# Prompt attention in a hybrid decoder step: TensorE's order written out by hand, value products of two steps in one run, probabilities turned in place, one ring of PSUM banks, and 640 keys cut as 384 and 256

## The chip, the cores and the metric

The program runs on one core of one Trainium2 chip. The metric is device time in microseconds (us) of one execution; the figure for the kernel before is the median of three runs. TensorE does the matrix products and the transposes, VectorE and ScalarE empty PSUM and do the softmax, GpSimd scales the probabilities in SBUF, and SyncE issues most of the transfers.

## The reference, cut to what matters

The reference is one layer of a decoder with 1024 prompt tokens and 32 sample tokens: input projections, sparse attention with an indexer, retention, and gated output products. What the change touches is the attention of the prompt and, in one line, the indexer's scores.

```python
def index_scores(qi, wi, ki):
    s = jnp.einsum('bqhd,bsd->bqhs', qi.astype(jnp.float32), ki.astype(jnp.float32))
    ...
    return jnp.einsum('bqhs,bqh->bqs', jax.nn.relu(s), w)

def sparse_attend(q, kg, vg, valid):
    logits = jnp.einsum('bqhd,bqkhd->bhqk', q, kg) * HEAD_DIM_A ** -0.5
    logits = jnp.where(valid[:, None], logits, -jnp.inf)
    p = jax.nn.softmax(logits, axis=-1)
    return jnp.einsum('bhqk,bqkhd->bqhd', p, vg)
```

Queries come in 8 blocks of 128, and block b sees (b + 1) * 128 keys. The kernel doesn't gather keys: it computes all logits of a block and adds a bias that masks those not selected.

## The kernel before, in words

The program is written with a tile framework that keeps the program's data dependences and chooses each engine's order itself, by a planner that simulates the program. `tc.issue_after(ins)` adds one constraint: what is traced inside the block and runs on the engine of `ins` comes after `ins`. All engines work through their order one by one, so an instruction that waits holds what stands behind it.

The stage of the change works on 4 pairs of heads `p`. For each, the 8 query blocks are taken in the order 7, 0, 6, 1 and 5, 2, 4, 3, two to a step, so that each step has 9 blocks of 128 keys for each of two heads. That makes 16 steps. A step has three parts.

- `logits` (L1319): for each block and head, the keys are cut in banks of up to 512 columns. Each bank takes two products (L1334 with the high part of the queries, L1335 with the low part) into a PSUM bank of the ring `lg` (three banks). VectorE adds the bias and keeps the running extreme (L1336), writing to the SBUF tile `lg` (three buffers); ScalarE takes the exponential with its row sum (L1342), VectorE the reciprocal (L1347), GpSimd scales in place (L1350). A generator yields after each bank: six to a step. 640 keys are cut as 512 and 128.
- `turn` (L1354): 18 transposes of 128x128 (L1362), four to a PSUM bank of the ring `tr` (two banks, for the last half step group also three of `lg`); ScalarE and VectorE copy each bank to an SBUF tile `pT` (L1365), every third copy on VectorE.
- `combine` (L1367): 18 products of turned probabilities with values, recorded as 36 instructions since fp32 products have two records each (L1380), 64 columns of the array for each head, into the bank `po` (one bank, kept for two steps). `together` ties them behind the first one. After every second step VectorE multiplies by the gate `za` (L1387) and splits the result in two parts (L1097, L1098).

Between these lies other work for TensorE: `from_retention` makes output products of the retention branch, 24 pieces of 12 products with 352 columns (L1131 to L1133) into a bank `pj` of two, and VectorE merges each piece (L1418). Five pieces are in the prologue, beside the logits of steps 0 and 1, one is left for after the last step.

In the loop over steps the program traces `turn`, for some steps a piece, the operand loads of the next pair, `combine`, the logits of the step two ahead, and one more piece up to step 11. The planner interleaves these on TensorE as their banks come free. PSUM holds 3 `lg`, 2 `tr`, 1 `po` and 2 `pj` banks.

After the stage, tiles `t` and `u` are loaded over the stage's freed SBUF (`load_merged`, L1471) and the attention branch's output products follow in the same pieces, merged on VectorE at L1520.

The indexer (L880 to L895) computes scores for blocks 7 to 2 in the first 130 us, four heads each, cut in banks of 512 and the rest (L887, L888), and ScalarE reads both banks at once (L890).

Of the kernel before, what the change touches and what calls it, by code (L numbers as in the profile page):

```python
# [8 lines left out]
F32 = mybir.dt.float32  # L9
# [3 lines left out]
AF = mybir.ActivationFunctionType  # L13
OP = mybir.AluOpType
# [5 lines left out]
T = 1024  # L20
# [104 lines left out]
def _hybrid_step(ctx, tc, A, outs, dbg):  # L125
    nc = tc.nc
# [24 lines left out]
    def pl():  # L151
        return ps.tile([128, 1024], F32, name="pl", bufs=2)
# [4 lines left out]
    def two():  # L157
        return [ps.tile([128, 512], F32, name="pb", bufs=3) for _ in (0, 1)]
# [26 lines left out]
    def together(products):  # L185

        last = first = products[0]()
        with tc.issue_after(first.ins):
            for f in products[1:]:
                last = f()  # L190
        return last
# [53 lines left out]
    def last_on(engine):  # L245
        return next(i for i in reversed(nc.cur_bb.bb.instructions) if i.engine == engine)
# [577 lines left out]
    with ExitStack() as s1:  # L824
# [4 lines left out]
        with ExitStack() as s2:  # L829
# [50 lines left out]
            for b in range(7, 1, -1):  # L880
                W = (b + 1) * 128
                for h in range(4):
                    p = pl()
                    for n0 in range(0, W, 512):
                        n1 = min(W, n0 + 512)
                        q = QS[h][:, b * 128:b * 128 + 128]
                        nc.tensor.matmul(p[:, n0:n1], q, KH[:, n0:n1], start=True, stop=False)  # L887
                        nc.tensor.matmul(p[:, n0:n1], q, KL[:, n0:n1], start=False, stop=True)  # L888
                    rl = ip.tile([128, LK], F32, name="rl", bufs=2)
                    nc.scalar.activation(rl[:, :W], p[:, :W], AF.Relu)  # L890
                    if h == 0:
                        nc.vector.tensor_scalar(SC[b], rl[:, :W], wsc[:, b, 0:1], None, op0=OP.mult)
                    else:
                        scored = nc.vector.scalar_tensor_tensor(SC[b], rl[:, :W], wsc[:, b, h:h + 1], SC[b], op0=OP.mult, op1=OP.add)
                if b == 7:  # L895
                    whole_row = scored.ins
                nc.vector.tensor_add(SC[b][:, W - 128:W], SC[b][:, W - 128:W], C[:, C_CAUS:C_CAUS + 128])
# [189 lines left out]
    def pbank(name, bufs):  # L1087
        return ps.tile([128, 512], F32, name=name, bufs=bufs)
# [6 lines left out]
    def parts(dst, src):  # L1095

        nc.scalar.copy(dst[0], src)  # L1097
        nc.vector.tensor_sub(dst[1], src, f32(dst[0]))  # L1098
# [59 lines left out]
    asked = {}  # L1158
# [160 lines left out]
    def logits(ap, step):  # L1319

        blocks, ops = step["blocks"], step["ops"][0]
        lg = step["lg"] = ap.tile([128, 2, 9 * 128], F32, name="lg", bufs=3)
        scaled_ = []
        c0 = 0
        for b in blocks:
            W = (b + 1) * 128
            qb = slice(b * 128, b * 128 + 128)
            st = ap.tile([128, 2, 4], F32, name="st", bufs=12)
            for i, (k, qh, ql) in enumerate(ops):
                l = lg[:, i, c0:c0 + W]  # L1330
                for n0 in range(0, W, 512):
                    n1 = min(W, n0 + 512)
                    x = pbank("lg", 3)
                    nc.tensor.matmul(x[:, :n1 - n0], qh[:, qb], k[:, n0:n1], start=True, stop=False)  # L1334
                    nc.tensor.matmul(x[:, :n1 - n0], ql[:, qb], k[:, n0:n1], start=False, stop=True)  # L1335
                    step["masked"] = nc.vector.tensor_tensor_reduce(  # L1336
                        out=l[:, n0:n1], in0=x[:, :n1 - n0], in1=BI[b][:, n0:n1], scale=-0.125,
                        scalar=-BIGNEG if n0 == 0 else st[:, i, 0:1], op0=OP.add, op1=OP.min,
                        accum_out=st[:, i, 0:1] if n1 < W else st[:, i, 1:2]).ins
                    if n1 < W:  # L1340
                        yield
                nc.scalar.activation(l, l, AF.Exp, bias=st[:, i, 1:2], scale=-1.0, accum_out=st[:, i, 3:4])  # L1342
                yield
            scaled_.append((st, c0, W))
            c0 += W
        for st, c0, W in scaled_:
            nc.vector.reciprocal(st[:, :, 2], st[:, :, 3])  # L1347
            for i in (0, 1):
                l = lg[:, i, c0:c0 + W]
                nc.gpsimd.tensor_scalar(l, l, st[:, i, 2:3], 0.5, op0=OP.mult, op1=OP.mult)  # L1350
# [3 lines left out]
    def turn(ap, step):  # L1354

        lg = step["lg"]
        PT = step["PT"] = []
        for j0 in range(0, 18, 4):
            m = min(4, 18 - j0)
            x = pbank("lg", 3) if step["p"] == 3 and step["group"][0] == 5 and j0 in (4, 8, 12) else pbank("tr", 2)  # L1360
            for j in range(j0, j0 + m):
                step["turned"] = nc.tensor.transpose(x[:, 128 * (j - j0):128 * (j - j0) + 128], lg[:, j % 2, 128 * (j // 2):128 * (j // 2) + 128], ident)  # L1362
            flip[0] += 1
            PT.append(ap.tile([128, 512], F32, name="pT", bufs=5))
            step["copied"] = (nc.vector.tensor_copy if flip[0] % 3 == 0 else nc.scalar.copy)(PT[-1][:, :128 * m], x[:, :128 * m])  # L1365

    def combine(ap, step):  # L1367

        (b0, b1), p, PT = step["blocks"], step["p"], step["PT"]
        ops, V, za = step["ops"]  # L1370
        if step["half"] == 0:
            step["po"][0] = pbank("po", 1)
        po = step["po"][0]

        slot = {b: i for i, b in enumerate(sorted(step["group"]))}
        run = [(b1, kb, b0 + 1 + kb) for kb in range(b1, -1, -1)] + [(b0, kb, kb) for kb in range(b0 + 1)]

        def product(b, kb, j, i):
            r = slice(64 * i, 64 * i + 64)
            return nc.tensor.matmul(po[r, 128 * slot[b]:128 * slot[b] + 128], V[:, kb, r], PT[j // 2][:, 256 * (j % 2) + 128 * i:256 * (j % 2) + 128 * i + 128],  # L1380
                                    start=(kb == (b if b == b1 else 0)), stop=(kb == (0 if b == b1 else b)))
        step["last"] = together([lambda b=b, kb=kb, j=j, i=i: product(b, kb, j, i) for b, kb, j in run for i in (1, 0)])
        if step["half"] == 1:
            pick = slice(0, 4, 3) if 0 in step["group"] else slice(1, 3)
            two = lambda t: t.rearrange("p (g c) -> p g c", c=256)[:, pick]
            y = ap.tile([128, 2, 256], F32, name="y", bufs=1)
            nc.vector.tensor_tensor(y, po.rearrange("p (g c) -> p g c", c=256), two(za), op=OP.mult)  # L1387
            parts((two(yah[:, p, :T]), two(yal[:, p, :T])), y)

    RT = dram.tile([D, TT], F32, name="RT")  # L1390

# [1 line left out]
    with ExitStack() as s4:  # L1393
# [4 lines left out]
        def operands(p):  # L1398
            if p not in loaded:
                loaded[p] = pair_operands(ap, p)  # L1400
            return loaded[p]
# [20 lines left out]

        for j in range(3):
            load_gate(j)
        steps = []
        for p in range(4):
            for group in ((7, 0, 6, 1), (5, 2, 4, 3)):
                po = [None]
                for half in (0, 1):
                    steps.append(dict(p=p, group=group, blocks=group[2 * half:2 * half + 2], half=half, po=po))  # L1430
        side = (x for j in range(KT) for x in from_retention(j))
        next(side)
        for step in steps[:2]:
# [8 lines left out]
                    next(side)  # L1442
            for _ in banks:
                pass
        for s_, step in enumerate(steps):
            if s_ == 4:
                nc.sync.dma_start(zs, by_pair(ZD))
                with tc.issue_after(step["masked"]):
                    nc.vector.tensor_tensor(YS, YS, zs, op=OP.mult)
                    parts((yah[:, :, T:], yal[:, :, T:]), YS)  # L1450
            turn(ap, step)
            if s_ >= 14 or s_ < 4:
                with tc.issue_after(step["turned"].ins):
                    next(side)
            if s_ % 4 == 0 and step["p"] + 1 < 4:
                with tc.issue_after(asked[3].ins):
                    operands(step["p"] + 1)
            combine(ap, step)
            if s_ + 2 < len(steps):
                steps[s_ + 2]["ops"] = operands(steps[s_ + 2]["p"])  # L1460
                for _ in logits(ap, steps[s_ + 2]):
                    pass
            with tc.issue_after(steps[max(s_ - 1, 0)]["last"].ins):
                for _ in zip(range(int(s_ <= 11)), side):
                    pass
        last = steps[-1]["last"]
    mp_ = ExitStack()
    mp = mp_.enter_context(tc.tile_pool(name="mp", bufs=1, side="right", reuse_waits="tile"))
    merged = {}
# [181 lines left out]
```

## Time and profile before

| | us |
|---|---|
| median of 3 runs | 1096.48 (1096.37 to 1097.05) |
| profiled execution, its own time | 1097.52 |
| its span, first to last instruction | 1095.7 |
| TensorE busy, matmuls | 1077.7 |
| VectorE busy | 669.9 |
| ScalarE busy | 468.7 |
| GpSimd busy | 230.0 |
| stage of the change (797.5 to 948.2 of the span) | 150.7 |

The profiled execution is 1.04 us above the median and lies 1.82 us above its own span. Matmuls are pipelined: a record is longer than the time after which the next one starts, so the distance between two starts is what a product costs, and a wait shorter than a record's end doesn't show as idle time.

### The profile page before, as it was taken

How to read it: one execution, taken by the hardware profiler on the slowest of the kernel's cores; microseconds unless marked ns; L12 is line 12 of the kernel's file. 1: busy time of each engine (PE TensorE's matmuls, PEld its weight loads, DVE VectorE, ACT ScalarE, POOL GpSimd, SP SyncE). 2: the span in 40 equal slices, each digit the busy share in tenths (PEclk: the TensorE clock that was granted, in tenths of full speed). 3: DMA queues.
4: the chain of work that ended last, by engine and by line, in shares of the span. 5: the costliest groups of instructions: out<-in, count | busy, mean ns of one | idle time of the engine just before them, and what ended most of it. 6: DMA issues, size and time to landing. Idle time of an engine off the chain costs nothing. (4 is left out here: it accounts for less than half of the span.)

```text
span 1095.7 us, 20456 instructions
## 1 busy us (share of the span) xinstructions
PE 1077.7 (98%) x8159; PEld 985.8 (90%) x8159; DVE 669.9 (61%) x1538; ACT 468.7 (43%) x925; POOL 230.0 (21%) x195
## 2 busy tenths in 40 slices
PE   7999999999999999999999999999999999999997
PEld 6899799999999989999999998888899998998776
DVE  6875269698887868999133222211266767497665
ACT  5675355455555555232244233311245666443211
POOL 0013025014321220020322222244122343100000
PEclk9999999999999999999999999999999999999999
DMA  9924344264254515522886758386887531457431
GB/s 296 265 73 126 95 118 138 84 197 127 80 161 128 157 47 184 156 83 100 289 278 206 240 168 248 122 286 228 311 296 239 188 114 31 144 187 249 163 116 58
DMA packets 156196, 185.64 MB, mean 169 GB/s; under 512 B 18740, under 2 KB 127172, under 8 KB 155012
## 3 DMA queue, kind: packets, MB, share of 16 engines
q1 hardware_dynamic: 145728, 147.81, 42.7%
q0 software_dynamic: 9856, 35.66, 9.7%
q8 instruction: 64, 1.05, 0.4%
q10 hardware_dynamic: 516, 0.86, 0.2%
q14 instruction: 32, 0.26, 0.1%
HBM read 139.34 MB, written 41.17 MB: 165 GB/s over the span
## 5 line engine op out<-in xcount | busy, mean ns | idle before, releaser
L226 PE MATMUL pj<-hh,wh 128*128 128x352 f32 (+1 forms) x1168 | 382.7, 328 | 0.0
L227 PE MATMUL pj<-hl,wh 128*128 128x352 f32 (+1 forms) x1168 | 378.8, 324 | 0.0
L228 PE MATMUL pj<-hh,wl 128*128 128x352 f32 (+1 forms) x1168 | 378.2, 324 | 0.2 <-POOL wl L212 0.2
L226 PEld LDWEIGHTS pj<-hh,wh 128*128 128x128 f32 x1168 | 219.3, 188 | 8.4 <-issue 7.1
L227 PEld LDWEIGHTS pj<-hl,wh 128*128 128x128 f32 x1168 | 219.8, 188 | 6.8 <-issue 6.0
L228 PEld LDWEIGHTS pj<-hh,wl 128*128 128x128 f32 x1168 | 219.4, 188 | 3.8 <-issue 3.2
L978 DVE TENSOR_SCALAR_CACHE_REDUCE eq<-sc,cand 128x896 bf16<-128x896 f32 (+4 forms) x155 | 135.7, 876 | 2.5
L211 ACT CAST wh<-ws 128x1024 fp32r<-128x1024 f32 (+1 forms) x65 | 61.0, 942 | 108.7 <-PE pj L227 88.4
L212 DVE TENSOR_TENSOR wl<-ws,wh 128x1024 fp32r<-128x1024 f32 (+1 forms) x47 | 54.5, 1162 | 44.3 <-ACT wh L211 44.0
L212 POOL TENSOR_TENSOR wl<-ws,wh 128x1024 fp32r<-128x1024 f32 x18 | 43.2, 2401 | 143.4 <-ACT wh L211 143.3
L1350 POOL TENSOR_SCALAR lg<-lg,st 128x1024 f32<-128x1024 f32 (+7 forms) x64 | 48.5, 775 | 113.1 <-DVE st L1347 102.1
L1342 ACT ACTIVATE lg<-lg,st 128x1024 f32<-128x1024 f32 (+7 forms) x64 | 49.3, 773 | 27.8 <-DVE st L1336 21.6
L1200 DVE COPY kt<-str 128x512 f32<-128x512 f32 x32 | 22.1, 690 | 63.4 <-PE str L1198 56.0
L1562 PE MATMUL pj<-woh,MH 128*128 128x512 f32 (+1 forms) x136 | 51.4, 378 | 0.0
L1563 PE MATMUL pj<-wol,MH 128*128 128x512 f32 (+1 forms) x136 | 51.2, 377 | 0.0
L1564 PE MATMUL pj<-woh,ML 128*128 128x512 f32 (+1 forms) x136 | 51.2, 377 | 0.0
L1167 POOL DMA_INDIRECT kv<-in_cache_k,idx x32 | 30.1, 939 | 95.0 <-PE str L1198 82.4
L1200 ACT COPY kt<-str 128x512 f32<-128x512 f32 x32 | 18.8, 587 | 64.0 <-PE str L1198 59.9
L816 ACT ACTIVATE raw<-pj 128x352 f32<-128x352 f32 x48 | 22.2, 463 | 47.8 <-PE pj L228 44.6
L1167 POOL DMA_INDIRECT kv<-in_cache_v,idx x32 | 31.4, 982 | 52.5 <-PE sx L1228 28.1
L1336 DVE CUSTOM_DVE_ANT_0 lg<-lg,bi 128x512 f32<-128x512 f32 (+3 forms) x64 | 36.4, 586 | 9.7 <-PE lg L1335 7.7
L1579 ACT ACTIVATE u<-xo 128x512 f32<-128x512 f32 (+2 forms) x19 | 11.6, 609 | 67.2 <-DVE xo L1578 44.7
(369 smaller groups left out, 1980.0 us busy)
## 6 DMA issues: line engine op xcount, KB each, us to landing
ws<-in_w_in SPq DMA_DIRECT2D x49, 512.0 KB
rot<-in_rot SPq DMA_DIRECT2D x8, 1056.0 KB
x<-in_w_ada SPq DMA_DIRECT2D x16, 512.0 KB
TG<-raw SPq DMA_DIRECT2D x15, 528.0 KB
wst<-in_w_out SPq DMA_DIRECT2D x12, 512.0 KB
u<-TG SPq DMA_DIRECT2D x8, 528.0 KB
t<-TG SPq DMA_DIRECT2D x8, 528.0 KB
x<-in_x_prompt SPq DMA_DIRECT2D x8, 512.0 KB
```

The lines of the kernel that those rows point to most:

```text
L211: nc.scalar.copy(wh[:, :, :n], ws[:, :, :n])
L212: (nc.vector if k == 4 or len(order) % 3 else nc.gpsimd).tensor_sub(wl[:, :, :n], ws[:, :, :n], f32(wh[:, :, :n]))
L226: nc.tensor.matmul(p, wh[:, k], HH[k][:, sl], start=(k == 0), stop=False)
L227: nc.tensor.matmul(p, wh[:, k], HL[k][:, sl], start=False, stop=False)
L228: nc.tensor.matmul(p, wl[:, k], HH[k][:, sl], start=False, stop=(k == KT - 1))
L978: nc.vector.tensor_scalar(junk[:n, :W], sc, thr[:n, j:j + 1], 0.0, op0=op, op1=OP.add, accum_out=cnt[:n, j:j + 1])
L1167: nc.gpsimd.indirect_dma_start(out=t.rearrange("p s c -> p (s c)"), out_offset=None, in_=cache.rearrange("g (r s) h d -> (g r) (s h d)", s ...
L1342: nc.scalar.activation(l, l, AF.Exp, bias=st[:, i, 1:2], scale=-1.0, accum_out=st[:, i, 3:4])
L1350: nc.gpsimd.tensor_scalar(l, l, st[:, i, 2:3], 0.5, op0=OP.mult, op1=OP.mult)
L1562: nc.tensor.matmul(x, MH[:, k, tk], wh[:, k], start=(k == 0), stop=False)
L1563: nc.tensor.matmul(x, MH[:, k, tk], wl[:, k], start=False, stop=False)
L1564: nc.tensor.matmul(x, ML[:, k, tk], wh[:, k], start=False, stop=(k == KT - 1))
```

## The change

It replaces the loop over 16 steps by one over 8 pairs of steps, in which every group of TensorE's instructions is traced in a block that puts it behind the last TensorE instruction traced so far (`in_line`). For pair g the order is: turn of its first step; the first three banks of logits of step 2g+2 (in g 0, 1 and 7 a retention piece before them); a piece; the other three banks; turn of its second step; the value products of both steps as one run; four banks of logits of step 2g+3; a piece (not in g 7); the other two banks.

`turn` puts two blocks of both heads in one bank and copies it back over the same columns of `lg`; the tile `pT` is gone, and `lg` is held until the run of value products has read it. Logits and transposes share one ring `x` of five banks. In `logits` 640 keys are cut as 384 and 256. In the indexer a width above 512 is cut in two equal halves. Of the diff only indentation and the unchanged lines of the masking are left out.

```diff
@@ indexer
-                    p = pl()
-                    for n0 in range(0, W, 512):
-                        n1 = min(W, n0 + 512)
-                        q = QS[h][:, b * 128:b * 128 + 128]
-                        nc.tensor.matmul(p[:, n0:n1], q, KH[:, n0:n1], start=True, stop=False)
-                        nc.tensor.matmul(p[:, n0:n1], q, KL[:, n0:n1], start=False, stop=True)
+                    m = -(-W // 512)
+                    p = pl().rearrange("p (m c) -> p m c", c=512)[:, :m, :W // m]
+                    q = QS[h][:, b * 128:b * 128 + 128]
+                    for n in range(m):
+                        sl = slice(n * W // m, (n + 1) * W // m)
+                        nc.tensor.matmul(p[:, n], q, KH[:, sl], start=True, stop=False)
+                        nc.tensor.matmul(p[:, n], q, KL[:, sl], start=False, stop=True)
-                    nc.scalar.activation(rl[:, :W], p[:, :W], AF.Relu)
+                    nc.scalar.activation(rl[:, :W].rearrange("p (m c) -> p m c", m=m), p, AF.Relu)
@@ logits
-                for n0 in range(0, W, 512):
-                    n1 = min(W, n0 + 512)
-                    x = pbank("lg", 3)
+                w = 384 if W == 640 else 512
+                for n0 in range(0, W, w):
+                    n1 = min(W, n0 + w)
+                    x = pbank("x", 5)
@@ turn
-        PT = step["PT"] = []
-        for j0 in range(0, 18, 4):
-            m = min(4, 18 - j0)
-            x = pbank("lg", 3) if step["p"] == 3 and step["group"][0] == 5 and j0 in (4, 8, 12) else pbank("tr", 2)
-            for j in range(j0, j0 + m):
-                step["turned"] = nc.tensor.transpose(x[:, 128 * (j - j0):128 * (j - j0) + 128], lg[:, j % 2, 128 * (j // 2):128 * (j // 2) + 128], ident)
+        for b0 in range(0, 9, 2):
+            m = min(2, 9 - b0)
+            x = pbank("x", 5)[:, :256 * m].rearrange("p (i c) -> p i c", i=2)
+            for i in (0, 1):
+                for b in range(m):
+                    step["turned"] = nc.tensor.transpose(x[:, i, 128 * b:128 * b + 128], lg[:, i, 128 * (b0 + b):128 * (b0 + b) + 128], ident)
             flip[0] += 1
-            PT.append(ap.tile([128, 512], F32, name="pT", bufs=5))
-            step["copied"] = (nc.vector.tensor_copy if flip[0] % 3 == 0 else nc.scalar.copy)(PT[-1][:, :128 * m], x[:, :128 * m])
+            (nc.vector.tensor_copy if flip[0] % 3 == 0 else nc.scalar.copy)(lg[:, :, 128 * b0:128 * (b0 + m)], x)
@@ combine: takes both steps of a pair
+        po = pbank("po", 1)
+        run = []
+        for step in pair:
+            b0, b1 = step["blocks"]
+            run += [(step, b1, kb, b0 + 1 + kb) for kb in range(b1, -1, -1)] + [(step, b0, kb, kb) for kb in range(b0 + 1)]
+        last = together([lambda a=a, i=i: product(*a, i) for a in run for i in (1, 0)])
@@ the loop
-        for s_, step in enumerate(steps):
...
-            turn(ap, step)
...
-            combine(ap, step)
...
+        def in_line(f):
+            with tc.issue_after(last_on(mybir.EngineType.PE)):
+                return f()
...
+        for g in range(8):
+            pair = steps[2 * g:2 * g + 2]
+            in_line(lambda: turn(ap, pair[0]))
+            if g % 2 == 0 and g < 6:
+                with tc.issue_after(asked[3].ins):
+                    operands(pair[0]["p"] + 1)
+            banks = score(2 * g + 2)
+            if g < 2 or g == 7:
+                piece()
+            in_line(lambda: some(banks, 3))
+            piece()
+            in_line(lambda: some(banks))
+            in_line(lambda: turn(ap, pair[1]))
...
+            last = in_line(lambda: combine(ap, pair))
+            banks = score(2 * g + 3)
+            in_line(lambda: some(banks, 4))
+            if g < 7:
+                piece()
+            in_line(lambda: some(banks))
```

Here `score(s)` starts the generator `logits` of step s (nothing past step 15), `some` draws banks from it, and `piece` draws one retention piece in line.

## Rows read from the trace of the kernel before

**Rows 1.** The page's first part: busy time of each engine over the whole span, its share, and the number of instructions.

```profile
PE 1077.7 (98%) x8159; PEld 985.8 (90%) x8159; DVE 669.9 (61%) x1538; ACT 468.7 (43%) x925; POOL 230.0 (21%) x195
```

**Rows 2.** Busy time by stretch: the stage of the change and the rest of the span after it. Columns: stretch, its length, busy us and number of instructions of PE, PEld, DVE, ACT and POOL, then the granted TensorE clock, the DMA share and GB/s.

```profile
797.50:948.20 150.70, 149.24 (x1334) 135.98 (x1332) 97.31 (x296) 86.84 (x198) 48.47 (x64) 1.00 0.45 154
948.20:1096.00 147.80, 139.90 (x776) 123.12 (x772) 105.35 (x240) 38.95 (x89) 0.00 (x0) 0.99 0.48 166
```

**Rows 3.** Timeline of TensorE around a turn of 8 transposes and the logits behind it. Columns: start, us until the last record's end, engine, line, operation, names, shape, number.

```profile
809.75 1.03 PE L1362 MATMUL tr<-C,lg 128*128 128x128 f32 x8
810.54 0.42 PE L1334 MATMUL lg<-kd,qh 128*128 128x384 f32 x1
810.80 0.34 PE L1335 MATMUL lg<-kd,ql 128*128 128x384 f32 x1
810.97 0.28 PE L1334 MATMUL lg<-kd,qh 128*128 128x256 f32 x1
811.09 0.28 PE L1335 MATMUL lg<-kd,ql 128*128 128x256 f32 x1
```

**Rows 4.** Timeline of TensorE where a bank of 512 columns is followed by one of 128 and then by a retention piece.

```profile
864.62 0.39 PE L1335 MATMUL lg<-kd,ql 128*128 128x512 f32 x1
864.85 0.22 PE L1334 MATMUL lg<-kd,qh 128*128 128x128 f32 x1
864.91 0.27 PE L1335 MATMUL lg<-kd,ql 128*128 128x128 f32 x1
865.02 0.38 PE L1131 MATMUL pj<-rh,wh 128*128 128x352 f32 x1
865.24 0.32 PE L1132 MATMUL pj<-rl,wh 128*128 128x352 f32 x1
865.40 0.33 PE L1133 MATMUL pj<-rh,wl 128*128 128x352 f32 x1
```

**Rows 5.** Timeline of TensorE around value products (L1380): a step whose run is cut in 4 and 32 records by one product of logits, a step with one run between two turns, and the start of the other step that is cut.

```profile
829.64 0.44 PE L1380 MATMUL po<-pT,V 128*64 128x128 f32 x4
830.01 0.50 PE L1334 MATMUL lg<-kd,qh 128*128 128x512 f32 x1
830.44 1.97 PE L1380 MATMUL po<-pT,V 128*64 128x128 f32 x32
832.34 0.51 PE L1335 MATMUL lg<-kd,ql 128*128 128x512 f32 x1
832.68 0.32 PE L1131 MATMUL pj<-rh,wh 128*128 128x352 f32 x1
...
879.01 0.60 PE L1362 MATMUL tr<-C,lg 128*128 128x128 f32 x4
879.54 2.19 PE L1380 MATMUL po<-pT,V 128*64 128x128 f32 x36
881.66 0.66 PE L1362 MATMUL tr<-C,lg 128*128 128x128 f32 x4
882.07 0.42 PE L1334 MATMUL lg<-kd,qh 128*128 128x384 f32 x1
...
921.16 0.44 PE L1380 MATMUL po<-pT,V 128*64 128x128 f32 x4
```

**Rows 6.** Whom TensorE waited for, over the whole span; the two rows of this stage. Columns: who, for whom, us in total, times, longest.

```profile
PE lg L1334 <- DVE st L1336: 1.2, 2, 0.6
PE po L1380 <- DVE pT L1365: 0.2, 1, 0.2
```

**Rows 7.** Groups of instructions of VectorE and ScalarE in the stage, shapes kept apart. Columns: line, engine, operation, names, shape, number, then busy us, mean ns of one, and the engine's idle time before them.

```profile
L1336 DVE CUSTOM_DVE_ANT_0 lg<-lg,bi 128x512 f32<-128x512 f32 x40 | 26.9, 685 | 8.3 <-PE lg L1335 6.5 <-PE tr L1362 0.8 <-POOL lg L1350 0.7
L1365 ACT COPY pT<-tr 128x512 f32<-128x512 f32 x39 | 22.3, 581 | 23.4 <-PE tr L1362 15.2 <-PE po L1380 6.7 <-DVE wl L212 1.4
L1365 DVE COPY pT<-tr 128x512 f32<-128x512 f32 x19 | 13.1, 687 | 5.1 <-PE tr L1362 5.1
L1342 ACT ACTIVATION_READ_ACCUMULATOR lg<-lg,st 128x1 f32 x64 | 12.0, 188 | 0.0
L1418 DVE SCALAR_TENSOR_TENSOR u<-u,pj 128x352 f32<-128x352 f32 x23 | 11.9, 518 | 12.8 <-PE pj L1133 12.6
L1342 ACT ACTIVATE lg<-lg,st 128x1024 f32<-128x1024 f32 x8 | 9.2, 1148 | 9.4 <-DMA TG<-raw 6.0 <-DVE st L1336 3.4
L1387 DVE TENSOR_TENSOR y<-po,za 128x512 f32<-128x512 f32 x7 | 4.8, 691 | 6.4 <-PE po L1380 6.4
L1098 DVE TENSOR_TENSOR yal<-y,yah 128x512 fp32r<-128x512 f32 x7 | 4.8, 686 | 0.4 <-ACT yah L1097 0.4
L1336 DVE CUSTOM_DVE_ANT_0 lg<-lg,bi 128x384 f32<-128x384 f32 x8 | 4.3, 553 | 1.0 <-PE lg L1335 1.0
L1336 DVE CUSTOM_DVE_ANT_0 lg<-lg,bi,st 128x256 f32<-128x256 f32 x8 | 3.8, 478 | 0.1
L1342 ACT ACTIVATE lg<-lg,st 128x128 f32<-128x128 f32 x8 | 3.1, 392 | 0.7 <-DVE st L1336 0.6
L1336 DVE CUSTOM_DVE_ANT_0 lg<-lg,bi,st 128x128 f32<-128x128 f32 x8 | 2.8, 347 | 2.1 <-PE lg L1335 1.8
```

**Rows 8.** Busy time, as in Rows 2, of the stretch near the end of the stage in which TensorE does 22 transposes one behind the other.

```profile
933.12:935.61 2.49, 2.49 (x23) 2.32 (x21) 1.93 (x7) 2.28 (x8) 1.76 (x3) 1.00 0.00 0
```

**Rows 9.** Around the end of the stage: SyncE's timeline, the first two loads of `t` (the second of them issued where the row ends), and VectorE's timeline, the first merge that reads them.

```profile
934.88 12.62 SPq L1473 DMA_DIRECT2D t<-TG  x2
...
954.40 0.95 DVE L1520 SCALAR_TENSOR_TENSOR t<-t,pj 128x352 f32<-128x352 f32 x2 [2.71 <-PE pj L1133]
```

More of the change, by code (lines that the diff above doesn't have):

```diff
@@ L1367, in combine @@
[L1367 to L1378, printed above, removed]
-            r = slice(64 * i, 64 * i + 64)
[L1380 to L1388, printed above, removed]
@@ new lines, in turn, with combine, product @@
+        for b0 in range(0, 9, 2):
[4 more added lines that the diff above has]
+                    step["turned"] = nc.tensor.transpose(x[:, i, 128 * b:128 * b + 128], lg[:, i, 128 * (b0 + b):128 * (b0 + b) + 128], ident)
+            flip[0] += 1
+            (nc.vector.tensor_copy if flip[0] % 3 == 0 else nc.scalar.copy)(lg[:, :, 128 * b0:128 * (b0 + m)], x)
+    def combine(ap, pair):
+        p, group = pair[0]["p"], pair[0]["group"]
+        ops, V, za = pair[0]["ops"]
+        po = pbank("po", 1)
+        slot = {b: i for i, b in enumerate(sorted(group))}
+        def product(step, b, kb, j, i):
+            r = slice(64 * i, 64 * i + 64)
+            return nc.tensor.matmul(po[r, 128 * slot[b]:128 * slot[b] + 128], V[:, kb, r], step["lg"][:, i, 128 * j:128 * j + 128],
+                                    start=(kb == (b if b == step["blocks"][1] else 0)), stop=(kb == (0 if b == step["blocks"][1] else b)))
+        run = []
[3 more added lines that the diff above has]
+        last = together([lambda a=a, i=i: product(*a, i) for a in run for i in (1, 0)])
+        y = ap.tile([128, 512], F32, name="y", bufs=1)
+        two = lambda t: t.rearrange("p (g c) -> p g c", c=256)[:, slice(0, 4, 3) if 0 in group else slice(1, 3)]
+        half = lambda t: t.rearrange("p (g c) -> p g c", c=256)
+        nc.vector.tensor_tensor(half(y), half(po), two(za), op=OP.mult)
+        parts((two(yah[:, p, :T]), two(yal[:, p, :T])), half(y))
+        return last
@@ L1424, in _hybrid_step @@
             load_gate(j)
[L1425 to L1430, printed above, removed]
+        steps = [dict(p=p, group=group, blocks=group[2 * half:2 * half + 2])
+                 for p in range(4) for group in ((7, 0, 6, 1), (5, 2, 4, 3)) for half in (0, 1)]
         side = (x for j in range(KT) for x in from_retention(j))
@@ L1444, in _hybrid_step, with score, some, piece @@
                 pass
-        for s_, step in enumerate(steps):
-            if s_ == 4:
+        def in_line(f):
+            with tc.issue_after(last_on(mybir.EngineType.PE)):
+                return f()
+        def score(s_):
+            if s_ < len(steps):
+                steps[s_]["ops"] = operands(steps[s_]["p"])
+                return logits(ap, steps[s_])
+            return iter(())
+        def some(banks, n=None):
+            for _ in banks if n is None else zip(range(n), banks):
+                pass
+        def piece():
+            in_line(lambda: next(side))
+        for g in range(8):
[11 more added lines that the diff above has]
+            in_line(lambda: turn(ap, pair[1]))
+            if g == 2:
                 nc.sync.dma_start(zs, by_pair(ZD))
-                with tc.issue_after(step["masked"]):
+                with tc.issue_after(steps[5]["masked"]):
                     nc.vector.tensor_tensor(YS, YS, zs, op=OP.mult)
                     parts((yah[:, :, T:], yal[:, :, T:]), YS)
-            turn(ap, step)
[L1452 to L1457, printed above, removed]
-            combine(ap, step)
[L1459 to L1466, printed above, removed]
+            last = in_line(lambda: combine(ap, pair))
[4 more added lines that the diff above has]
+            in_line(lambda: some(banks))
     mp_ = ExitStack()
```

## The prediction

> **What bounds the kernel now.** I read the page's first part first: TensorE is 98% busy and no other engine is above 61% [rows 1]. Next came busy time by stretch: in the stage of the change TensorE is busy 149.24 of 150.70 us, VectorE 97.31, ScalarE 86.84, GpSimd 48.47, at a granted clock of 1.00 [rows 2]. The chain of waits isn't of use: it is TensorE from end to end. But a busy TensorE isn't one at its best pace, since records overlap. So I went to its timeline in the stage, took the distance between starts as the price of a product, and looked for distances that are longer than others of the same shape. The reader should do the same. What TensorE saves here comes off the end: behind the stage it goes on at 139.90 of 147.80 us [rows 2].
>
> Paces: a product of 352 columns takes 0.16 us (865.24 to 865.40), of 512 0.23 (864.62 to 864.85) [rows 4], of 384 0.17 and of 256 0.12 (810.80, 810.97, 811.09) [rows 3]. Eight transposes take 0.79 until the next product starts; that one then takes 0.26 where 384 columns cost 0.17, so eight are 0.79 + 0.09 = 0.88, or 0.11 each, and a change from turning to logits costs nothing besides [rows 3]. Value products: 4 records take 0.37 (829.64 to 830.01), 32 take 1.90 (830.44 to 832.34), so one is (1.90 - 0.37) / 28 = 0.055 and a run has 0.15 on top [rows 5].
>
> Work at these paces: 23 pieces of 12 products, 276 x 0.16 = 44.2; 16 x 18 transposes x 0.11 = 31.7; 16 x 36 value records x 0.055 = 31.7; logits, from the cuts of the code (96 products of 512, 32 each of 384, 256 and 128, the last at half of 256), 22.1 + 5.4 + 3.8 + 1.9 = 33.2. Sum 140.8 of 150.7 [rows 2]. So 9.9 us are neither, and the change can give at most these.
>
> **Value products in 8 runs, not 18.** Sixteen steps have a run each and two of them are cut in two [rows 5]. Price of a run: 0.15 inside; on the way in 0.09, as four transposes ahead of one take 0.53 (879.01 to 879.54) where 4 x 0.11 = 0.44; on the way out 0.11 into a product (832.34 to 832.68 is 0.34, not 0.23), or 0.06 into a turn (881.66 to 882.07 is 0.41, where four transposes and the borrowed 0.09 make 0.35) [rows 5]. That is 0.30 to 0.35. Before: mostly into turns, 18 x 0.30 = 5.4. After: always from a turn into a product, 8 x 0.35 = 2.8. **Gain 2.6.** The second product of logits in the cut step shows both borders at once: 830.01 to 830.44 is 0.43, 0.20 over its pace [rows 5].
>
> **640 keys as 384 and 256.** A bank of 128 columns costs 0.06 + 0.11 and makes the next product 0.06 late (0.22, not 0.16): 0.23 in all, where linear pace asks 0.12 [rows 4]. That is 0.11 for each of 8 such banks (4 pairs x 2 heads); the 8 of block 0 stay. As 384 + 256 the pair costs 2 x (0.17 + 0.12) = 0.58, as 512 + 128 at linear pace also 0.58. **Gain 0.85.** VectorE: 685 + 347 = 1032 ns against 553 + 478 = 1031, nothing [rows 7]. In the indexer the same cut (512 + 128) stands four times, in block 4, and goes too: 0 to 0.4, since its products aren't all on the same line; I take 0.2. Blocks 5 and 6 have the same columns in other halves. ScalarE's read in two pieces isn't in the trace; the product with `za` in two halves takes 691 ns beside 687 for a plain copy of as many, so nothing [rows 7].
>
> **Turned in place.** As many transposes, as many copies. The copy now writes two runs of 256: by the same two rows it costs nothing, at most 0.01 each. `lg` is held longer, until the value products end; the third buffer covers one step ahead, and the step two ahead draws its buffer only behind that run on TensorE, so no wait is added that TensorE's order doesn't already hold. Freed `pT` buffers take a wait away.
>
> **One ring of five, order by hand.** It removes what I see as waits: 1.2 us for the ring of three logits banks and 0.2 of a value run for a copy [rows 6]. **Gain 1.4.** What is left of the 9.9: 9.9 - 5.4 - 16 x 0.11 - 1.4 = 1.3 in short delays below a record's end and in rounding. I leave it as it is, as the price of a fixed order that the planner can no longer fill: new waits of the same 1.3, net nothing. This is the choice on which most hangs, and its bounds come from two places in every pair.
>
> First place: the turn that follows a pair's run, four banks, a piece and two banks. For blocks 4 and 3 TensorE needs 4 x 0.29 + 1.93 + 4 x 0.23 + 18 x 0.11, about 6.0 us. VectorE must in that time do the gate product 0.69, masks 2 x (0.55 + 0.48) + 2 x 0.69 = 3.4, the split 0.69 and a merge 0.52: 5.3 us [rows 7]. The ring lends five banks, so it fits with little left. Queued behind the turn, if its fourth or fifth bank is late: logits and a piece, which need nothing of it.
>
> Second place: the run of value products. Its second half needs the second turn's copies, the last bank first. From the turn's start TensorE is busy 2.0 + 2.0 us with the turn and the first step's products. ScalarE may have the last exponentials of the logits just done in front (1.15 + 0.19 and 2 x (0.39 + 0.19), together 2.5 us) and then up to four copies at 0.58: 4.8 us [rows 7]. So TensorE is late by nothing if copies come first and by up to some 0.8 if exponentials do. Eight pairs: 0 to 6.4 us; I take the lower part because in the trace such a run waited for a copy only 0.2 us in all [rows 6], though it had a shorter lead there.
>
> The Trainium skill, "PSUM — Partial Sum Buffer", section "Engine vs sequencer instructions", says that ScalarE and VectorE take their queues strictly in order. By that, a copy that the planner puts behind an exponential cannot pass it, however early its bank is full; this is the rival below that ends on the other side.
>
> **Queues.** SyncE's loads keep their order: the next pair's operands are asked after the first turn of an even g, one pair ahead of need. The zs load and product move into g 2, beside a piece. Loads of `t` after the stage lie over its SBUF: before, the second left at 947.5, after the last value run, and the first merge that reads `t` was at 954.40, after TensorE's pieces [rows 9]. With `lg` held to the last run the first may also leave only then. That is 6 us ahead of its reader: 0 to 1, I take 0.
>
> **Sum.** 2.6 + 0.85 + 0.2 + 1.4 = 5.05, taken as 5.0. Against the profiled execution: 1097.5 - 5.0 = 1092.5; the median of the runs is 1.04 below that execution, so 1091.5. Bounds of the unknown: +1.3 more if nothing new waits, +0.2 indexer, and some 0.7 for the paces' rounding: 1089.3. The other way, 6.4 of late copies less what I have left in (1.3) is 5.1 and would eat all; three quarters of the gain is what I let the range give back beside the tail's 1: 1096.3.
>
> **Rivals.**
> 1. *The gain is eaten.* The value runs and cuts give 3.65, but TensorE waits 0.5 to 0.9 us in each pair at the second place. Time 1094.3 to 1098.7, centre 1096. For it: the 4.8 against 4.0 us. Against it: copies are ready before exponentials whose masks are still running. Chance 0.15.
> 2. *Slower: an exponential in front of a copy holds the ring.* After the first turn of a pair, three logits banks follow with no piece between them in g 2 to 6, and each needs a copied bank. If ScalarE has both late exponentials of the last block in front of the copies (0.72 to 1.34 each with its read), TensorE stands, and the planner can't put a piece there any more. It decides from 0.9 us a pair (8 x 0.9 = 7.2, past 5.0 + 2.2). At 1.3 for one exponential of 1024 at each pair's start: 8 x 1.3 = 10.4 - 5.0, so 1102. Against it: ScalarE is busy 86.84 of 150.70 us [rows 2], so a lag doesn't build up. Chance 0.07.
> 3. *The runs aren't what they say.* If other products still cut the runs or the order costs as much as 18 runs did, 2.6 goes: 1094. It is inside the forecast's range, 0.05 of its chance.
> 4. *The clock.* Transposes now come 18 in a row. In the trace 22 in a row ran at a granted clock of 1.00 [rows 8], so no loss. The Trainium skill, "TensorE: Matmul & The Clock Gate", section "Part 4: PE-mode transpose", says transposes don't count as TensorE being busy in the same way; by it the clock might fall to half there. If it did, 16 turns of 2.0 us would take 32 more, time 1124. The row speaks against it. Chance 0.01.
>
> **Chances.** A run of this kernel can tell about 0.2%, 2.2 us, from no change. Faster than 1094.3: 0.76 (the forecast with its bounds). Same: 0.16 (rival 1 and the tail). Slower than 1098.7: 0.08 (rivals 2 and 4).
>
> **What would show it.** In TensorE's timeline of the changed kernel: 8 rows of 72 value records, each 4.1 us until the next start; no product of 128 columns but those of block 0; 16 rows of 18 transposes with 1.9 to 2.0 each; the stage about 145.7 us long. TensorE's waits on VectorE's masks gone from the list; if instead it waits on ScalarE's or VectorE's copies into `lg` for more than 5 us in all, rival 1 or 2 holds. The stretch behind the stage should keep its length of 148 us; if it grows, a load was late. I am wrong if the runs cost less than 0.30 (gain too large) or if the fixed order waits above 0.6 us a pair.

## The result, and the profile after

The changed kernel takes 1090.26 us (median of 6, 1090.12 to 1091.06) against 1096.38 (median of 6): a ratio of 0.9948, interval 0.9938 to 0.9959, 6.1 us less. I had forecast 1091.5 and a range of 1089.3 to 1096.3. The profiled execution took 1091.06, with a span of 1089.3. The medians of e3 and e5 further down leave out one run each that lies far off the others, 1780.61 us at a granted clock of 0.56 and 5455.66 us.

The page's first part of the changed kernel: TensorE's busy time falls by 4.6 us, its share is as near to full as before [rows 1], so it says little on where the time went.

```profile
PE 1073.1 (99%) x8159; PEld 988.1 (91%) x8159; DVE 666.8 (61%) x1538; ACT 466.5 (43%) x925; POOL 228.8 (21%) x195
```

Busy time by stretch of the changed kernel, columns as in [rows 2]: the stage, then the rest.

```profile
796.60:941.90 145.30, 145.08 (x1335) 137.52 (x1334) 94.53 (x297) 84.68 (x198) 47.15 (x64) 1.00 0.46 156
941.90:1089.40 147.50, 139.74 (x772) 123.03 (x772) 105.29 (x240) 39.08 (x89) 0.00 (x0) 0.99 0.49 169
```

The stage is 145.3 us long and was 150.7; the rest has its length still [rows 2]. A sharper ruler for all runs is one row of the view of the tile `rh`, the first and last start of the retention pieces' first product, since five pieces stand ahead of the stage's loop and one behind it. First before, then changed; columns: line, engine, operation, names, number, ns least/median/most, first and last start.

```profile
L1131 PE MATMUL pj<-rh,wh x96: 317/323/427, 797.6 to 949.8; 128*128 128x352 f32 x96
```

```profile
L1132 PE MATMUL pj<-rh,wh x96: 318/323/427, 796.6 to 943.3; 128*128 128x352 f32 x96
```

That is 152.2 us before and 146.7 after: **5.5 us come from the stage.** The 1.0 us by which the stage begins earlier is mostly the execution's own: in the runs below it begins between 795.1 and 798.3, and the runs at both these ends have nothing different ahead of it from the changed kernel.

TensorE's timeline of one pair in the changed kernel, to be read against [rows 3, 5]; columns as there.

```profile
853.71 2.13 PE L1364 MATMUL x<-C,lg 128*128 128x128 f32 x18
855.77 4.19 PE L1377 MATMUL po<-lg,V 128*64 128x128 f32 x72
859.89 0.45 PE L1336 MATMUL x<-kd,qh 128*128 128x384 f32 x1
860.17 0.34 PE L1337 MATMUL x<-kd,ql 128*128 128x384 f32 x1
860.35 0.29 PE L1336 MATMUL x<-kd,qh 128*128 128x256 f32 x1
```

Eighteen transposes take 2.06, which is 0.08 over 18 x 0.11; 72 value records take 4.12, 0.16 over 72 x 0.055; the first product behind takes 0.28, not 0.17. That is 0.35 for a run, and there are eight. The block of 640 keys now begins with 384 and goes on with 256.

Whom TensorE waited for in the stage: of [rows 6] nothing is left, and one row is new.

```profile
PE po L1377 <- ACT lg L1366: 0.2, 1, 0.2
```

It stands where I had put the second place. ScalarE's timeline of the changed kernel there, then TensorE's:

```profile
837.57 0.59 ACT L1366 COPY lg<-x 128x512 f32<-128x512 f32 x1 [0.90 <-PE x L1364]
838.05 1.15 ACT L1344 ACTIVATE lg<-lg,st 128x1024 f32<-128x1024 f32 x1
...
839.20 0.39 ACT L1344 ACTIVATE lg<-lg,st 128x128 f32<-128x128 f32 x1
...
839.58 0.39 ACT L1344 ACTIVATE lg<-lg,st 128x128 f32<-128x128 f32 x1
...
839.96 1.32 ACT L1366 COPY lg<-x 128x512 f32<-128x512 f32 x3
```

```profile
836.85 2.15 PE L1364 MATMUL x<-C,lg 128*128 128x128 f32 x18
838.93 2.19 PE L1377 MATMUL po<-lg,V 128*64 128x128 f32 x36
841.34 2.19 PE L1377 MATMUL po<-lg,V 128*64 128x128 f32 x36 [0.22 <-ACT lg L1366]
```

The planner put one copy ahead of the three exponentials and three behind them; the last copy ends at 841.28 and the second half starts at 841.34, 2.41 after the first where 36 x 0.055 is 1.98. This is the worst of the eight pairs; one other is 0.13 late by its starts and six are not late.

The list of waits counts idle time only. The two waits for masks of the kernel before [rows 6], in its timeline:

```profile
803.39 0.28 PE L1335 MATMUL lg<-kd,ql 128*128 128x128 f32 x1
804.31 0.33 PE L1334 MATMUL lg<-kd,qh 128*128 128x128 f32 x1 [0.65 <-DVE st L1336]
...
927.06 0.27 PE L1335 MATMUL lg<-kd,ql 128*128 128x128 f32 x1
927.85 0.50 PE L1334 MATMUL lg<-kd,qh 128*128 128x512 f32 x1 [0.51 <-DVE st L1336]
```

From start to start they are 0.92 and 0.79 where the pace is 0.11: 1.5 us late, not 1.2. Added up over all distances in the stage that are more than 0.07 over the prediction's paces, the borders of value runs left out, TensorE was late by 2.7 us before and is by 0.8 in the changed kernel. Below, "late by starts" means this sum.

Around the end of the stage, SyncE's timeline and VectorE's, against [rows 9]:

```profile
939.96 0.80 SPq L1489 DMA_DIRECT2D t<-TG  x2
```

```profile
947.85 0.95 DVE L1536 SCALAR_TENSOR_TENSOR t<-t,pj 128x352 f32<-128x352 f32 x2 [2.67 <-PE pj L1134]
```

Both loads of `t` left before the last value run had ended, not behind it, 7 us ahead of their reader. What ended the merge's wait was TensorE.

### The profile page after: what moved, and what is told of

It is laid out like the page before. It is cut to its first block, busy times and chain, and to the rows that moved or that the text cites. A ratio compares the mean times of both kernels' runs of the same rounds, so it can differ in the third digit from the quotient of the medians.

```text
span 1089.3 us, 20448 instructions
## 1 busy us (share of the span) xinstructions
PE 1073.1 (99%) x8159; PEld 988.1 (91%) x8159; DVE 666.8 (61%) x1538; ACT 466.5 (43%) x925; POOL 228.8 (21%) x195
## 5 line engine op out<-in xcount | busy, mean ns | idle before, releaser
L1344 ACT ACTIVATE lg<-lg,st 128x128 f32<-128x128 f32 (+7 forms) x64 | 49.5, 774 | 29.7 <-DVE st L1338 29.7
L986 ACT ACTIVATE ra<-scs,cand 32x1056 bf16<-32x1056 f32 x31 | 36.4, 1175 | 0.8
```

## The experiments

Lengths are from the row of `rh`, last start minus first, in one profiled execution of each; times are medians with the ratio to the kernel before, run beside it.

| run | time, us | ratio (interval) | length, us |
|---|---|---|---|
| before | 1096.38 | | 152.2 |
| changed | 1090.26 | 0.9948 (0.9938 to 0.9959) | 146.7 |
| e1, cut of 640 alone | 1095.33 | 0.9990 (0.9981 to 0.9999) | 151.4 |
| e2, ring of five alone | 1096.26 | 1.0001 (0.9992 to 1.0010) | 152.4 |
| e3, changed without the order by hand (length of e8, the same kernel) | 1105.13 | 1.0083 (1.0069 to 1.0097) | 161.5 |
| e4, changed with two runs a pair | 1093.54 | 0.9974 (0.9965 to 0.9984) | 149.8 |
| e5, changed with the ring split 3 and 2 | 1119.94 | 1.0225 (1.0206 to 1.0243) | 175.5 |
| e6, changed, all copies on ScalarE | 1099.74 | 1.0034 (1.0021 to 1.0047) | 155.8 |
| e7, indexer's cut alone | 1095.40 | 0.9993 (0.9984 to 1.0002) | 152.2 |
| e9, changed, turned out of place | 1090.59 | 0.9946 (0.9933 to 0.9960) | 146.8 |
| e10, changed with a ring of four | 1096.87 | 1.0008 (0.9999 to 1.0017) | 153.1 |
| e11, changed, late copies on VectorE | 1089.65 | 0.9942 (0.9929 to 0.9956) | 146.3 |

**e1, the cut of 640 alone**, on the kernel before.

```diff
-                for n0 in range(0, W, 512):
-                    n1 = min(W, n0 + 512)
+                w = 384 if W == 640 else 512
+                for n0 in range(0, W, w):
+                    n1 = min(W, n0 + w)
```

> The kernel before with the cut of 640 keys as 384 and 256 alone, in the logits. My theory (a bank of 128 columns costs TensorE 0.11 us more than its columns): 8 such banks fewer, 0.85 us less than before, nearly all in the stage; no product of 128 columns left but those of block 0. Rival (the planner fills or hides it, or only reorders): within 0.3 us of before.

Measured: the stage is 0.8 us shorter, the median 1.1. The theory holds; nothing hid it.

**e2, one ring of five alone**, on the kernel before.

```diff
-                    x = pbank("lg", 3)
+                    x = pbank("x", 5)
@@ turn
-            x = pbank("lg", 3) if step["p"] == 3 and step["group"][0] == 5 and j0 in (4, 8, 12) else pbank("tr", 2)
+            x = pbank("x", 5)
```

> The kernel before with one ring of five banks for logits and transposes, and nothing else; the planner still chooses the order. My theory (TensorE's waits for VectorE's masks came from the ring of three): the 1.2 us of waits for masks go, 1 to 1.5 us less than before, value runs still 16 to 18 at 0.30 each. Rival (the waits come from the planner's order, not from the number of banks): as many waits in other places, within 0.5 us of before or slower.

Measured: 1.0001, the stage 0.2 longer. The waits for masks of [rows 6] did go, and one for a copy came (TensorE's waits of e2, the only row of this stage):

```profile
PE x L1334 <- DVE pT L1365: 0.8, 1, 0.8
```

But the planner now cuts value products in six steps, not in two [rows 5]; one of the six:

```profile
939.21 0.44 PE L1380 MATMUL po<-pT,V 128*64 128x128 f32 x4
939.58 0.44 PE L1362 MATMUL x<-C,lg 128*128 128x128 f32 x2
```

Counted over its timeline there are 22 runs, not 18. TensorE is late by 1.3 us by starts, 1.4 less than before, and four more runs at 0.30 to 0.35 are 1.2 to 1.4. So the time is the rival's, and my theory was right on the masks' waits and wrong on the number of runs: with the planner's order the ring nets nothing, since what it frees goes into more cuts.

**e3 and e8, the changed kernel without the order by hand.**

```diff
         def in_line(f):
-            with tc.issue_after(last_on(mybir.EngineType.PE)):
-                return f()
+            return f()
```

> The changed kernel without the hand-written order: the blocks that put each group behind the last TensorE instruction are taken out, the rest is as changed (value products of two steps in one run, turned in place, one ring, new cuts). My theory (the order by hand nets about nothing; the runs, the cuts and the ring carry the gain): within 1 us of the changed kernel. Rival (the order by hand carries most of it, since the planner breaks runs and makes TensorE wait): 3 to 6 us slower than the changed kernel, so near the kernel before.

Measured: 1105.13, 14.9 us slower than the changed kernel and 9 slower than the one before. My theory falls by far; the rival had the side right and not the size. e8 is the same kernel, and its expectation names the cause that I then held.

> The changed kernel without the hand-written order once more, for a profile. My theory, now: what makes it slow are value runs cut in pieces by the planner; at 0.34 us each some 47 pieces in place of 8 are 13 us of the 15 that it lost. Rival: the pieces are few and the time stands as waits for copies or masks.

TensorE's timeline of e8 in the middle of one pair's values:

```profile
839.81 0.43 PE L1377 MATMUL po<-lg,V 128*64 128x128 f32 x2
840.17 0.66 PE L1364 MATMUL x<-C,lg 128*128 128x128 f32 x4
840.76 0.88 PE L1377 MATMUL po<-lg,V 128*64 128x128 f32 x12
```

Two value records take 0.36 (839.81 to 840.17) where 2 x 0.055 is 0.11. Counted over its timeline, the values come in 47 pieces, not 8: `together` ties products behind the first, and the planner fills whatever is ready between them. 39 more at 0.30 (into a turn) to 0.34 are 11.7 to 13.3 of the 14.8 us by which its stage is longer. The rest is in the size of the pieces: two records alone take as long as four, 0.36 and 0.37 (829.64 to 830.01 in [rows 5]), so 0.055 holds only where the products of both heads alternate, and a product without one of the other head beside it costs 0.11 more. 20 of the 47 pieces end with such a one: 2.2 us. The rival's waits are few: its list has 0.7 us in the stage. Its time (1104.44 in one run) agrees with e3.

**e4, two runs a pair again.**

```diff
-            last = in_line(lambda: combine(ap, pair))
             banks = score(2 * g + 3)
-            in_line(lambda: some(banks, 4))
+            last = combine(ap, pair, lambda: in_line(lambda: some(banks, 3)))
+            in_line(lambda: some(banks, 1))
```

Here `combine` does each step's products in line and calls its third argument between the two.

> The changed kernel with the value products of a pair cut in two runs again, three banks of the next logits between them (in the last pair there are none, so 7 more runs). My theory (a run costs 0.34 to 0.35 us wherever it stands): 7 x 0.35 = 2.4 us slower than the changed kernel. Rival (the gain of the run came from waits that the longer lead removes, not from the switch): under 1 us slower, or the added time stands as waits and not at the borders of the runs.

TensorE's timeline of e4, the same pair as shown of the changed kernel:

```profile
856.39 2.19 PE L1377 MATMUL po<-lg,V 128*64 128x128 f32 x36
858.50 0.45 PE L1336 MATMUL x<-kd,qh 128*128 128x384 f32 x1
858.79 0.34 PE L1337 MATMUL x<-kd,ql 128*128 128x384 f32 x1
...
859.39 0.34 PE L1337 MATMUL x<-kd,ql 128*128 128x384 f32 x1
859.66 2.19 PE L1377 MATMUL po<-lg,V 128*64 128x128 f32 x36
861.77 0.39 PE L1336 MATMUL x<-kd,qh 128*128 128x256 f32 x1
862.00 0.28 PE L1337 MATMUL x<-kd,ql 128*128 128x256 f32 x1
```

Each run takes 2.11 (0.13 over 36 x 0.055); behind each the first product is 0.11 late (0.29 of 384 columns, 0.23 of 256), and the one ahead of the second run takes 0.27, not 0.17. One run more is 0.13 + 0.10 + 0.11 = 0.34, as priced. The stage is 3.1 us longer: 7 x 0.34 = 2.4 at the borders, as in my theory, and 0.7 that I hadn't expected. These are waits: logits behind a turn are late by 1.5 by starts at two places (0.4 in its list, for a copy), and the 0.8 of the changed kernel is gone.

**e5, the ring split again**, on the changed kernel: `pbank("lg", 3)` in `logits`, `pbank("tr", 2)` in `turn`.

> The changed kernel with the ring of five split again: three banks for logits, two for transposes, the order still by hand. My theory (the fixed order needs the shared ring, since it has nothing to put between a turn's banks): each turn of five banks waits for the copies of its first banks, 0.57 us on ScalarE or 0.69 on VectorE where four transposes take 0.44, so some 0.5 to 1 us for each of 16 turns, 8 to 16 us slower than the changed kernel and slower than before. Rival (the ring is worth what its removal was worth in the planner's order, about nothing): within 1.5 us of the changed kernel.

Measured: the stage is 28.8 us longer, 1.8 a turn, nearly twice the upper end. The waits of e5, and TensorE's timeline at the last turn, where ScalarE has no exponential left to do:

```profile
PE tr L1364 <- ACT lg L1366: 10.1, 21, 0.8
PE tr L1364 <- DVE lg L1366: 7.4, 12, 0.9
```

```profile
963.48 1.04 PE L1364 MATMUL tr<-C,lg 128*128 128x128 f32 x8
964.81 1.14 PE L1364 MATMUL tr<-C,lg 128*128 128x128 f32 x8 [0.29 <-ACT lg L1366]
966.25 0.44 PE L1364 MATMUL tr<-C,lg 128*128 128x128 f32 x2 [0.30 <-DVE lg L1366]
966.62 4.15 PE L1377 MATMUL po<-lg,V 128*64 128x128 f32 x72
```

The side is as expected, the size not. This turn takes 3.14 us (963.48 to 966.62) where the changed kernel takes 2.06, so 1.1 a turn is lost to two banks and the copies alone, a little over my upper end. The 16 turns take 3.14 to 4.10, 3.6 in the mean; the three longest, 4.0 to 4.1, are those in which ScalarE has an exponential of 1024 columns between its copies, which I had not counted. Some 3 us more lie outside the turns.

**e6, all copies on ScalarE**, on the changed kernel: `nc.scalar.copy` for every bank of a turn.

> The changed kernel with all copies of turned banks on ScalarE, none on VectorE. My theory (the second half of a pair's value products has no lead left over ScalarE's exponentials and copies): one or two more copies of 0.57 us stand in front, so 0.5 to 1.1 us of wait in each of 8 pairs at the middle of the run, 4 to 9 us slower than the changed kernel. Rival (ScalarE has slack, busy 84.7 of 145.3 us): under 1 us slower.

Measured: the stage is 9.1 us longer, the upper end. The waits of e6, and TensorE's timeline at the second place:

```profile
PE po L1377 <- ACT lg L1366: 3.8, 7, 0.7
...
PE x L1336 <- DVE st L1338: 2.3, 5, 0.5
```

```profile
839.15 2.19 PE L1377 MATMUL po<-lg,V 128*64 128x128 f32 x36
842.05 2.19 PE L1377 MATMUL po<-lg,V 128*64 128x128 f32 x36 [0.71 <-ACT lg L1366]
```

The wait stands where the theory has it, in the middle of the run: 5.0 us by starts in seven pairs, 0.5 to 0.9 each. That the sum came to the upper end is chance, since logits are late by 4.5 more, which the theory didn't have. The list puts their waits down to VectorE's masks; I read them as ScalarE's copies, which is argued and not shown: by the ring's order the bank that the third logits bank behind a turn takes is the turn's third, and at one such place ScalarE and TensorE do this:

```profile
869.03 1.34 ACT L1366 COPY lg<-x 128x512 f32<-128x512 f32 x3
```

```profile
869.67 0.50 PE L1336 MATMUL x<-kd,qh 128*128 128x512 f32 x1 [0.43 <-DVE st L1338]
```

**e7, the indexer's cut alone**: the diff's first part on the kernel before.

> The kernel before with the indexer's new cut alone. My theory: 4 banks of 128 columns fewer at 0.05 to 0.11 us, 0.2 to 0.4 us less, below what the times can tell; in the trace the distance from before at the products of 140 us is 0.2 to 0.4 us. Rival (the planner's order up to the stage carries the whole 1.0 us that the changed kernel is ahead there): 1 us less than before where the stage begins.

The transposes of the indexer's past keys frame most of its blocks; one row of the view of `kx`, before and then e7:

```profile
L939 PE MATMUL pt<-C,kx x32: 270/273/295, 89.2 to 130.4; 128*128 128x128 f32 x32
```

```profile
L940 PE MATMUL pt<-C,kx x32: 271/272/273, 87.9 to 128.9; 128*128 128x128 f32 x32
```

41.2 us against 41.0: 0.2, and the stage has its old length. From the first of these transposes to the last of all that read `kx`, far behind the indexer, it is 518.3 to 518.4 us in the three traces with the old cut (before, e1, e2) and 518.0 to 518.1 in the nine with the new: 0.2 to 0.4. By its median alone nothing can be said. The stage begins 1.0 earlier than before, as the rival has it, but not for the cut: e7 is 1.3 ahead already at the first of these transposes, and the changed kernel, which has the same cut, is not (89.1).

**e9, turned out of place**, on the changed kernel.

```diff
+            pT = ap.tile([128, 512], F32, name="pT", bufs=10)
...
-            (... nc.scalar.copy)(lg[:, :, 128 * b0:128 * (b0 + m)], x)
+            (... nc.scalar.copy)(pT[:, :256 * m].rearrange("p (i c) -> p i c", i=2), x)
... (the value products read pT)
@@ logits
-        lg = step["lg"] = ap.tile([128, 2, 9 * 128], F32, name="lg", bufs=3)
+        lg = step["lg"] = ap.tile([128, 2, 9 * 128], F32, name="lg", bufs=2)
```

> The changed kernel with the turned probabilities in tiles of their own again (ten buffers of 2 KB, since both steps of a pair are held), and two buffers of the logits in place of three, which is what SBUF has room for. My theory (the copy costs the same wherever it writes, and the order holds the waits already): within 0.5 us of the changed kernel, the copies at 0.57 to 0.58 us on ScalarE and 0.69 on VectorE as in place. Rival (writing two runs of 256 over the tile, or holding the logits longer, costs time): 1 us or more faster than the changed kernel.

Measured: 146.8 against 146.7. Copies of e9 by shape, as in [rows 7]:

```profile
L1368 ACT COPY pT<-x 128x512 f32<-128x512 f32 x43 | 23.7, 575 | 4.8 <-PE x L1364 4.8
L1368 DVE COPY pT<-x 128x512 f32<-128x512 f32 x21 | 14.4, 687 | 2.9 <-PE x L1364 2.5
```

The changed kernel's copies of these shapes take 573 and 688 ns. Turning in place neither costs nor gains time, with one logits buffer less in e9. It saves SBUF: ten tiles of 2 KB against one buffer of 9.

**e10, a ring of four**, on the changed kernel: `pbank("x", 4)` in both places.

> The changed kernel with a shared ring of four banks in place of five. My theory (a turn needs its five banks without a wait; with two it lost 1.6 us each): the fifth bank of a turn waits for the first one's copy only where an exponential is in front of it, and the logits behind a turn need the second and later copies 0.4 us earlier: 1 to 5 us slower than the changed kernel. Rival (four are as good): within 0.5 us.

Measured: the stage is 6.4 us longer and the whole gain is gone. A turn in e10's timeline:

```profile
854.23 1.03 PE L1364 MATMUL x<-C,lg 128*128 128x128 f32 x8
855.55 1.35 PE L1364 MATMUL x<-C,lg 128*128 128x128 f32 x10 [0.29 <-DVE st L1338]
```

Here eight transposes take 1.32, not 0.88, since the third bank waits for a mask of the logits ahead. I had looked for waits for copies; those for masks, the first place, came on top: in the second to fourth banks of the turns TensorE is late by 2.1 us in all, in the fifth, which needs the turn's own first copy, by 1.5, and the rest lies in the logits behind.

**e11, the late copies on VectorE**, on the changed kernel.

```diff
... (turn takes on_vector)
-            flip[0] += 1
-            (nc.vector.tensor_copy if flip[0] % 3 == 0 else nc.scalar.copy)(lg[:, :, ...], x)
+            (nc.vector.tensor_copy if b0 // 2 in on_vector else nc.scalar.copy)(lg[:, :, ...], x)
@@ the loop
-            in_line(lambda: turn(ap, pair[0]))
+            in_line(lambda: turn(ap, pair[0], (2,)))
-            in_line(lambda: turn(ap, pair[1]))
+            in_line(lambda: turn(ap, pair[1], (1, 3, 4)))
```

> The changed kernel with the copies dealt out by place: of a pair's first turn only the third bank on VectorE, of its second turn the second, fourth and fifth (4 of 10 in place of 3.3). My theory (the waits that are left stand before the second half of the value runs, for copies that ScalarE has behind its exponentials while VectorE idles): the 0.7 us of such waits go, 0.5 to 0.9 us faster than the changed kernel, unless the first turn's copies make the logits wait. Rival (VectorE's masks then come late and the ring waits for them): 0.5 us or more slower.

TensorE's timeline of e11 at the place shown of the changed kernel:

```profile
835.34 2.15 PE L1364 MATMUL x<-C,lg 128*128 128x128 f32 x18
837.42 4.15 PE L1376 MATMUL po<-lg,V 128*64 128x128 f32 x72
```

The run is whole, without the wait in its middle. The stage is 0.4 us shorter than that of the changed kernel, less than I expected. It is the fastest of all, 1089.65, but its interval overlaps that of the changed kernel, so the times don't tell the two apart.

## Why the prediction was right, point by point

**The bound.** TensorE's distances were the right place to look: the tail kept its length, and 5.5 of the 6.1 us came out of the stage. The other 0.6 are the indexer's 0.2 to 0.4 (e7) and what executions differ by.

**Value products in 8 runs: 2.6.** Right. A run costs 0.35 in the changed kernel and 0.34 in e4, and the 39 more runs of e8 fit that price.

**640 keys: 0.85, indexer 0.2.** Right: 0.8 (e1) and 0.2 to 0.4 (e7).

**Turned in place: nothing.** Right (e9).

**One ring of five, order by hand: gain 1.4, new waits as large as the old rest, net nothing.** This is the step that was mis-sized. Of the 5.5 us, 2.6 and 0.85 are taken, so ring and order gave 2.05, not 1.4. The 1.4 was read off the list of waits, though a wait under a record's end doesn't show there: by starts TensorE was late by 2.7 before, and the list's 1.4 was half of it. And the new waits that I took to be as large as the old rest of 1.3 are 0.8, all waits together. 2.7 less 0.8 is 1.9 of the 2.05.

I also took the order for a cost only, and had no word on what it is for: without it the planner cuts the pair's run in pieces and the change as a whole is slower than before (e3, e8), and what the ring frees goes into more cuts (e2). The order in turn needs the ring: split it costs 28.8 us (e5), one bank less 6.4 (e10). So the 2.05 can't be shared out between ring and order, and the 2.6 is had only where the order keeps the runs whole. That the forecast's total came near although it gave the order no worth is luck in part: the change happened to hold all that its terms needed. No run has the order by hand alone on the kernel before.

**The two places.** Right as mechanisms. Exponentials do stand in front of copies, and the worst pair was late by 0.43, about half of the bound's 0.8: of the up to four copies that I had put behind the exponentials, one ran ahead of them (837.57). e6 makes this place lose 5.0 us and the kernel slower than before, e11 takes it away. The first place was nearer the edge than I wrote: with a bank less (e10) it makes a third of a loss of 6.4 us.

**Rivals.** The gain was not eaten, and no exponential held the ring: the list has 0.2 us of waits in the stage. The runs cost what the forecast gave them. The Trainium skill, "PSUM — Partial Sum Buffer", section "Engine vs sequencer instructions", has ScalarE's queue strictly in order; the trace agrees: the three copies begin at 839.96, right behind the exponentials that stand ahead of them, although the transposes' last record had ended at 839.00. The clock rival fell: with 18 transposes in a row the granted clock of the stage is 1.00.

**Queues.** I feared that the loads of `t` might leave only behind the last run; they left before its end.

## What to carry to other kernels

A run of products that use 64 columns of the array for each head, between other work, has a price beside its products (here 0.34 us): count the runs in the timeline before counting products, and make sure that the planner can't cut one. Whether the column tiling makes the price or the two records of an fp32 product, no run here tells apart. An order fixed by hand, the banks that it needs and the engines that empty them are one change: taken in pieces, each piece looked worthless or harmful here. Where a run's second half depends on copies, see whether the engine that makes them has longer work in front, and give them to the one that idles (0.4 us of the stage here, e11).

## What the runs showed of the hardware that I had not expected

- One bank more or less decides: with five shared banks TensorE waited 0.2 us in the list, with four the stage is 6.4 us longer, with three and two 28.8.
- Two value records alone, between other work, take 0.36 us (e8), more than three times what they take in a run, and as long as four (0.37): cut runs, and not waits, make e8 slower than the kernel before.
